# Feed-forward input blocks: hi and lo side by side as 512 moving columns, and 512-column lo pieces

## The chip, the cores and the metric

The kernel runs on one core of one Trainium2 chip. The time is the device time of one execution in microseconds (us); times of the kernel before are a median of three executions, and one further execution was profiled.

## What is computed

A sequence of 256 tokens with 1024 features, `x[256,1024]`, goes through 16 sub-layers, all in 32-bit floating point. Ten of them are feed-forward layers: eight gated ones with inner width 2816 (four) or 2752 (four), and two plain ones with inner width 4096. The others are six token mixers (a convolution, a gated linear recurrence, three kinds of attention, a pooling mixer).

```python
def swiglu_ffn(x, w_in, w_out):                      # 4 times (f00, f01, f10, f11), D_FF = 2816
    gate, up = jnp.split(x @ w_in, 2, axis=-1)
    return (jax.nn.silu(gate) * up) @ w_out

def swiglu(h, w_gate, w_up, w_down):                 # 4 times (g00, g01, g10, g11), D_FF_2 = 2752
    return (jax.nn.silu(h @ w_gate) * (h @ w_up)) @ w_down

...
x = x + jnp.square(jax.nn.relu(u @ w_ff1[i])) @ w_ff2[i]   # twice (m0, m1), width 4096
```

Between them stand the norms, the modulation by `ada_w` (its rows are called ada jobs below) and the residual sums.

## The kernel before

**Numbers.** Each fp32 factor is kept as two rounded parts, hi and lo, and a product is three matmuls: hi x hi, hi x lo and lo x hi. All weights lie in one DRAM tensor as chunks of [128, 2048] (1 MB), in the order of their use. `_load` fetches a chunk on SP's DMA queue into one of three `raw` buffers; `_split` makes `hi` on ACT (L330, four pieces of 512 columns) and `lo = raw - hi` on VectorE (DVE; L335). For the chunks of the feed-forward layers the lo comes in eight pieces of 256 columns (`LP = 8`), for all others in four of 512. There are five `hi` and five `lo` buffers, so a chunk can be split up to four chunks ahead of its use. The input of a layer lies transposed in two tiles `xh` and `xl` of [128, 8, 256]: features on the partitions, 8 slices of 128, 256 tokens.

**A feed-forward layer (`ffn`).** It has 22 input chunks U(f), each with the columns of gate and up for 128 hidden features, and 11 output chunks V(g). The first four U chunks are done by `first` into the four PSUM banks a0 to a3. The blocks f = 4 to 21 go through `u_products`: for the gate half and the up half (b = 0, 1) and each slice k there are three matmuls of 256 moving columns, in which the weights are the stationary factor and the input moves: `wh.xh` (L552), `wh.xl` (L553), `wl.xh` (L554). All 48 go into one PSUM bank, gate in the first half of it and up in the second, from the tag `ps` of two banks. `hidden` then empties the bank: Silu of the gate half on ACT (L733), times the up half on DVE (L734), and the split of the product into `hh` (ACT, L735) and `hl` (DVE, L736). In block f = 4, after the 40th matmul, `turn` puts in 8 transposes (L760) of the first four blocks' results, into two banks of the tag `tr` (also two banks), which `split` empties (L697, L698). After f = 5 the output products begin (`down`, L622, 512 moving columns of V, `hh` and `hl` stationary): V(0) and V(1) after f = 5, then one V after every second block to f = 15; the last six U blocks run back to back, and the last four V chunks follow in `finish`.

**A plain layer (`mlp`).** The same with 12 blocks through `proj_u` (which calls `u_products`), then Relu, square and split (L798, L799, L697, L698).

**Order.** The Tile framework places the instructions of each engine in a row at build time, by its own scheduling; on the chip each engine works off its row in order, and waits at its head. What follows an instruction in ACT's or DVE's row therefore waits with it. The ada jobs are 144 operations of DVE (L1159), strewn over seven of the gated layers.

Of the kernel before, what the change touches and what calls it, by code (L numbers as in the profile page):

```python
# [12 lines left out]
F32R = mybir.dt.float32r  # L13
# [278 lines left out]

class _K:
    RB, HB = 3, 5
    HP, LP = 4, 8

    def __init__(self, nc, tc, a, plan, stages, ctx):
        self.nc, self.tc, self.a, self.plan, self.stages, self.ctx = nc, tc, a, plan, stages, ctx
# [22 lines left out]
    def _split(self):  # L321
        i = self.nsplit
        while self.nload <= i:
            self._load()
        r = self.raws.pop(i)
        h = self.hi_p.tile([128, 2048], F32R, name="hi")
        l = self.lo_p.tile([128, 2048], F32R, name="lo")
        for p in range(self.HP):
            c = slice(2048 // self.HP * p, 2048 // self.HP * (p + 1))
            self.nc.scalar.activation(h[:, c], r[:, c], AF.Copy)  # L330

        lp = self.LP if self.plan[i][1][0] in "fg" or self.plan[i][1] in ("m0", "m1") else self.LP // 2
        for p in range(lp):
            c = slice(2048 // lp * p, 2048 // lp * (p + 1))
            self.nc.vector.tensor_tensor(l[:, c], r[:, c], h[:, c].bitcast(F32), op=OP.subtract)  # L335
        self.his[i], self.los[i] = h, l
        self.nsplit += 1
# [194 lines left out]
    def new_act(self):  # L532

        if self.the_act is None:
            self.the_act = (self.act.tile([128, 8, 256], F32R, name="xh"), self.act.tile([128, 8, 256], F32R, name="xl"))
        return self.the_act


# [6 lines left out]
    def u_products(self, w, act, p, nb=2):  # L545
        wh, wl = w
        xh, xl = act
        for b in range(nb):
            o = p[:, 256 * b:256 * b + 256]
            for k in range(8):  # L550
                c = slice(256 * k + 128 * b, 256 * k + 128 * b + 128)
                yield self.nc.tensor.matmul(o, lhsT=wh[:, c], rhs=xh[:, k, :], start=(k == 0), stop=False)  # L552
                yield self.nc.tensor.matmul(o, lhsT=wh[:, c], rhs=xl[:, k, :], start=False, stop=False)  # L553
                yield self.nc.tensor.matmul(o, lhsT=wl[:, c], rhs=xh[:, k, :], start=False, stop=(k == 7))  # L554

    def proj_tile(self, w, act, p, m, at):
        wh, wl = w
# [144 lines left out]
    def ffn(self, s, act):  # L702
        nc, tc = self.nc, self.tc
        nf = 22
        with tc.tile_pool(name="hp_" + s, bufs=2) as hp:
# [12 lines left out]
            def hidden(f, p):  # L718
                g, b = divmod(f, 2)
                if b == 0:  # L720
                    groups[g] = (hp.tile([128, 2, 256], F32R, name="hh", bufs=4), hp.tile([128, 2, 256], F32R, name="hl", bufs=4))
                hh, hl = groups[g]
                ragged = s[0] == "g" and f == nf - 1
                if ragged:

                    for t in (hh, hl):
                        nc.gpsimd.memset(t[64:, b].bitcast(F32), 0.0)
                n = 64 if ragged else 128
                gate = p[:n, :256]
                upp = p[64:128, :256] if ragged else p[:, 256:]  # L730
                sg = hp.tile([128, 256], F32, name="sg")
                h = hp.tile([128, 256], F32, name="h")
                nc.scalar.activation(sg[:n], gate, AF.Silu)  # L733
                nc.vector.tensor_tensor(h[:n], sg[:n], upp, op=OP.mult)  # L734
                nc.scalar.activation(hh[:n, b], h[:n], AF.Copy)  # L735
                nc.vector.tensor_tensor(hl[:n, b], h[:n], hh[:n, b].bitcast(F32), op=OP.subtract)  # L736

# [16 lines left out]

            def turn():
                for g in range(2):
                    p = self.ps("tr")
                    for b in range(2):
                        for m in range(2):
                            nc.tensor.transpose(p[:, 256 * b + 128 * m:256 * b + 128 * m + 128], hts[2 * g + b][:, m], self.ident)  # L760
                    groups[g] = self.split(p, hp)
# [3 lines left out]
            for g in range(2, 11):  # L765
                for f in (2 * g, 2 * g + 1):
                    w = self.take(("U", s, f))
                    if f > 4:
                        more()
                    p = self.ps()  # L770
                    products = self.u_products(w, act, p, 1 if s[0] == "g" and f == nf - 1 else 2)
                    if f == 4:
                        self.issue(products, 40, turn)
                    else:
                        self.issue(products)
                    hidden(f, p)
                    if f == 5:
                        acc = self.new_acc()
                    for j in ((0, 1) if f == 5 else (g - 1,) if f % 2 and g < 8 else ()):
                        w = self.take(("V", s, j))  # L780
                        more()
                        for m in range(2):
                            self.down(m, acc[m], w, hs(j), (128, 128), j == 0, False)
# [6 lines left out]
    def mlp(self, s, act):  # L790
        nc, tc = self.nc, self.tc
        with tc.tile_pool(name="hp_" + s, bufs=2) as hp:
            groups = {}

            def hidden(g, p):
                r = hp.tile([128, 512], F32, name="sg")
                h = hp.tile([128, 512], F32, name="h", bufs=1)
                nc.scalar.activation(r, p, AF.Relu)  # L798
                nc.vector.tensor_tensor(h, r, r, op=OP.mult)  # L799
                groups[g] = self.split(h, hp)  # L800

            hs = lambda g: [(groups[g][0][:, b], groups[g][1][:, b]) for b in range(2)]
            p4 = self.first(s, ((0, 1), (2, 3)), act)
            for g in range(4):
                r = hp.tile([128, 2, 256], F32, name="sg")
                h = hp.tile([128, 2, 256], F32, name="h", bufs=1)
                for m in range(2):
                    nc.scalar.activation(r[:, m], p4[g][m], AF.Relu)
                    nc.vector.tensor_tensor(h[:, m], r[:, m], r[:, m], op=OP.mult)
                groups[g] = self.split(self.turn4(h).rearrange("p b t -> p (b t)"), hp)  # L810
            acc = self.new_acc()
            self.rows_ahead(s)
            for g in range(2, 16):
                if g > 3:
                    hidden(g, self.proj_u(self.take(("U", s, g)), act))
                if g < 14:
                    w = self.take(("V", s, g - 2))
                    for m in range(2):
                        self.down(m, acc[m], w, hs(g - 2), (128, 128), g == 2, False)
            held = [(self.take(("V", s, g), g - 12), hs(g), (128, 128)) for g in (12, 13, 14, 15)]  # L820
            return self.finish(acc, held, self.cur_post)
# [1013 lines left out]
```

## Time and profile before

| | us |
|---|---|
| median of three executions | 2630.83 (2629.59 to 2634.77) |
| the profiled execution, its own time | 2628.67 |
| span of the profiled execution | 2626.9 |
| PE (TensorE matmul) busy | 2585.0 (98%) |
| DVE busy | 1914.4 (73%) |
| ACT busy | 1374.9 (52%) |

Spans and waits below are of the profiled execution. An operation's duration (mean ns of one) runs from its start to its end; successive operations on an engine overlap, so what one costs in a row of many is the distance from start to start. That distance is called pitch here, and it is shorter than the duration.

### The profile page before, as it was taken

To read this page: it belongs to the slowest core of one execution; us is meant where nothing else is said; L and a number is where in the kernel's file an instruction comes from. 1 tells how busy PE (TensorE), PEld (TensorE's weight loads), DVE (VectorE), ACT (ScalarE), POOL (GpSimd) and SP (SyncE) were. 2 spreads that over 40 slices of the span, in tenths; PEclk is the share of its full clock that TensorE was granted. 3 is DMA by queue.
4 is the path that set the end of the run, shared out by engine and by line. 5 is a ranking of instruction groups with operands and counts; after the bars stand their busy time and mean duration, and the time that the engine had idled before them with its cause. 6 is when DMAs were issued, how large, how long until landed. Compare 5 with 4: busy or idle time off the path is not lost.

```text
span 2626.9 us, 43032 instructions
## 1 busy us (share of the span) xinstructions
PE 2585.0 (98%) x15958; PEld 2286.7 (87%) x15958; DVE 1914.4 (73%) x5151; ACT 1374.9 (52%) x3037; POOL 71.6 (3%) x158
## 2 busy tenths in 40 slices
PE   8999999999999999999999999999999999999999
PEld 7998889989998899899779989977899788977898
DVE  7858587587578875985878778677855866577754
ACT  5545454454545544644664454466644655466543
POOL 0000000000000000000000000000100000000000
PEclk9999999999999999999999999999999999999999
DMA  8847376486425675784548768653555545542552
GB/s 325 305 161 281 145 259 246 150 331 233 169 92 194 258 288 177 279 307 175 177 162 303 264 230 332 219 210 129 210 191 177 187 162 197 187 170 97 192 182 91
DMA packets 92739, 554.53 MB, mean 211 GB/s; under 512 B 10717, under 2 KB 11757, under 8 KB 38385
## 3 DMA queue, kind: packets, MB, share of 16 engines
q1 hardware_dynamic: 92528, 551.79, 57.4%
q8 instruction: 125, 2.05, 0.3%
q14 instruction: 86, 0.70, 0.1%
HBM read 550.62 MB, written 1.13 MB: 210 GB/s over the span
## 4 chain that ended last, share of the span: by engine, by line
PE 58%; issue 34%; DVE 3%; ACT 2%; POOL 1%; DMA 1%; SPq 0%; POOLq 0%; ACTq 0%; DVEq 0%
PE a L622 20%; PE ps L552 8%; PE ps L553 8%; PE ps L554 8%; PE a L581 2%; PE a L583 2%; PE a L582 2%; DVE lo L335 2%; PE a L903 1%; PE tr L503 1%; DMA raw<-in_wall 1%; POOL ry L447 1%; ACT hi L330 1%; ACT junk L441 1%; PE a L1303 0%
## 5 line engine op out<-in xcount | busy, mean ns | idle before, releaser
L335 DVE TENSOR_TENSOR lo<-raw,hi 128x256 fp32r<-128x256 f32 (+1 forms) x2964 | 1158.1, 448 | 387.3 <-ACT hi L330 386.8
L330 ACT ACTIVATE hi<-raw 128x512 fp32r<-128x512 f32 x1652 | 944.3, 623 | 759.2 <-issue 271.3
L552 PE MATMUL ps<-xh,hi 128*128 128x256 f32 x2784 | 789.9, 284 | 0.0
L553 PE MATMUL ps<-xl,hi 128*128 128x256 f32 x2784 | 788.5, 283 | 0.0
L554 PE MATMUL ps<-xh,lo 128*128 128x256 f32 x2784 | 788.2, 283 | 0.0
L553 PEld LDWEIGHTS ps<-xl,hi 128*128 128x128 f32 x2784 | 533.4, 192 | 3.6
L552 PEld LDWEIGHTS ps<-xh,hi 128*128 128x128 f32 x2784 | 533.3, 192 | 3.6
L554 PEld LDWEIGHTS ps<-xh,lo 128*128 128x128 f32 x2784 | 533.4, 192 | 0.1
L622 PE MATMUL a<-hi,hh 128*128 128x512 f32 x960 | 309.6, 396 | 0.0
L622 PE MATMUL a<-lo,hh 128*128 128x512 f32 x960 | 309.3, 396 | 0.0
L622 PE MATMUL a<-hi,hl 128*128 128x512 f32 x960 | 309.3, 396 | 0.0
L622 PEld LDWEIGHTS a<-lo,hh 128*128 128x128 f32 x960 | 179.9, 188 | 43.7
L622 PEld LDWEIGHTS a<-hi,hl 128*128 128x128 f32 x960 | 179.9, 187 | 43.5
L1159 DVE SCALAR_TENSOR_TENSOR adaj<-adaw,cond 128x1024 bf16<-128x1024 f32 x144 | 175.6, 1219 | 42.8 <-DMA adaw<-in_ada 41.6
L622 PEld LDWEIGHTS a<-hi,hh 128*128 128x128 f32 x960 | 174.5, 188 | 36.2 <-ACT hh L697 0.2
L581 PE MATMUL a<-hi,xh 128*128 128x512 f32 x512 | 201.4, 394 | 3.2 <-ACT xh L511 1.8
L583 PE MATMUL a<-hi,xl 128*128 128x512 f32 x512 | 201.9, 396 | 0.6 <-DVE xl L512 0.6
L582 PE MATMUL a<-lo,xh 128*128 128x512 f32 x512 | 200.1, 391 | 0.3 <-DVE lo L335 0.3
L581 PEld LDWEIGHTS a<-hi,xh 128*128 128x128 f32 x512 | 96.6, 189 | 26.5 <-ACT xh L516 5.4
L583 PEld LDWEIGHTS a<-hi,xl 128*128 128x128 f32 x512 | 96.3, 188 | 24.7 <-DVE xl L512 3.2
L582 PEld LDWEIGHTS a<-lo,xh 128*128 128x128 f32 x512 | 96.6, 189 | 20.6 <-DVE lo L335 0.8
L735 ACT ACTIVATE hh<-h 128x256 fp32r<-128x256 f32 x144 | 59.1, 410 | 71.9 <-DVE h L734 71.9
(364 smaller groups left out, 2607.5 us busy)
## 6 DMA issues: line engine op xcount, KB each, us to landing
raw<-in_wall SPq DMA_DIRECT2D x413, 1024.0 KB, 4.8
adaw<-in_ada SPq DMA_DIRECT2D x144, 512.0 KB, 6.8
taps<-in_ctaps SPq DMA_DIRECT2D x10, 1024.0 KB, 7.8
G<-in_rows SPq DMA_DIRECT2D x16, 512.0 KB, 5.7
pg<-in_rows SPq DMA_DIRECT2D x12, 512.0 KB, 4.9
xn<-modd SPq DMA_DIRECT2D x12, 512.0 KB
cond<-condd SPq DMA_DIRECT2D x7, 512.0 KB, 6.1
memt<-in_mem SPq DMA_DIRECT2D x4, 512.0 KB, 3.3
```

The lines of the kernel that those rows point to most:

```text
L330: self.nc.scalar.activation(h[:, c], r[:, c], AF.Copy)
L335: self.nc.vector.tensor_tensor(l[:, c], r[:, c], h[:, c].bitcast(F32), op=OP.subtract)
L441: self.nc.scalar.activation(j, src, AF.Square, scale=1.0 / 32, accum_out=st[:, n:n + 1])
L552: yield self.nc.tensor.matmul(o, lhsT=wh[:, c], rhs=xh[:, k, :], start=(k == 0), stop=False)
L553: yield self.nc.tensor.matmul(o, lhsT=wh[:, c], rhs=xl[:, k, :], start=False, stop=False)
L554: yield self.nc.tensor.matmul(o, lhsT=wl[:, c], rhs=xh[:, k, :], start=False, stop=(k == 7))
L581: yield self.nc.tensor.matmul(p, lhsT=xh[:, k, t], rhs=wh[:, c], start=(k == 0), stop=False)
L582: yield self.nc.tensor.matmul(p, lhsT=xh[:, k, t], rhs=wl[:, c], start=False, stop=False)
L583: yield self.nc.tensor.matmul(p, lhsT=xl[:, k, t], rhs=wh[:, c], start=False, stop=(k == 7))
L622: mm = lambda l, r, i, st, sp: nc.tensor.matmul(acc[i], lhsT=l[:k, t], rhs=r[:k, 1024 * b + 512 * i:1024 * b + 512 * i + 512], start=st, s ...
L735: nc.scalar.activation(hh[:n, b], h[:n], AF.Copy)
L1159: self.nc.vector.scalar_tensor_tensor(junk, self.ada_w.pop(n), 1.0, self.cond, op0=OP.mult, op1=OP.mult, accum_out=self.mods[k][:, c:c + 1])
```

## The change

`xh` and `xl` become the two halves of one tile `both` of [128, 8, 2, 256], so that for each slice k the 512 columns [hi | lo] lie side by side. `wide_products` takes the place of `u_products` in the feed-forward blocks f = 4 to 21 and in the 12 blocks of each plain layer: for each half b and slice k one matmul of 512 moving columns, `wh` stationary (into the whole bank: the first 256 columns collect hi x hi, the others hi x lo), and one of 256 columns, `wl.xh`, into the first half of the bank. Gate and up therefore need a bank each: gate takes one of `ps`, up takes one of `tr`. `added` joins the halves of a bank: ACT copies the second to SBUF, DVE adds the first. `hidden` then works on SBUF: Silu (L754 in the new kernel), product (L756), split. The second bank of `turn` comes from `ps`, and `turn` stands after the 26th of now 32 products. The lo split is four pieces of 512 columns for every chunk. The blocks of the convolution, the recurrence and the first attention that go through `u_products` keep it.

```diff
--- before.py
+++ after.py
@@ -292,7 +292,7 @@
 class _K:
     RB, HB = 3, 5
-    HP, LP = 4, 8
+    HP, LP = 4, 4
     def __init__(self, nc, tc, a, plan, stages, ctx):
         self.nc, self.tc, self.a, self.plan, self.stages, self.ctx = nc, tc, a, plan, stages, ctx
@@ -328,8 +328,7 @@
         for p in range(self.HP):
             c = slice(2048 // self.HP * p, 2048 // self.HP * (p + 1))
             self.nc.scalar.activation(h[:, c], r[:, c], AF.Copy)
-
-        lp = self.LP if self.plan[i][1][0] in "fg" or self.plan[i][1] in ("m0", "m1") else self.LP // 2
+        lp = self.LP
         for p in range(lp):
             c = slice(2048 // lp * p, 2048 // lp * (p + 1))
             self.nc.vector.tensor_tensor(l[:, c], r[:, c], h[:, c].bitcast(F32), op=OP.subtract)
@@ -532,7 +531,8 @@
     def new_act(self):
         if self.the_act is None:
-            self.the_act = (self.act.tile([128, 8, 256], F32R, name="xh"), self.act.tile([128, 8, 256], F32R, name="xl"))
+            self.both = self.act.tile([128, 8, 2, 256], F32R, name="xh")
+            self.the_act = (self.both[:, :, 0], self.both[:, :, 1])
         return self.the_act
@@ -552,6 +552,28 @@
                 yield self.nc.tensor.matmul(o, lhsT=wh[:, c], rhs=xh[:, k, :], start=(k == 0), stop=False)
                 yield self.nc.tensor.matmul(o, lhsT=wh[:, c], rhs=xl[:, k, :], start=False, stop=False)
                 yield self.nc.tensor.matmul(o, lhsT=wl[:, c], rhs=xh[:, k, :], start=False, stop=(k == 7))
+
+    def wide_products(self, w, p):
+
+
+        wh, wl = w
+        mm = self.nc.tensor.matmul
+        for b, o in enumerate(p):
+            for k in range(8):
+                c = slice(256 * k + 128 * b, 256 * k + 128 * b + 128)
+                x = self.both[:, k]
+                hi = lambda start, stop: mm(o, lhsT=wh[:, c], rhs=x.rearrange("p i t -> p (i t)"), start=start, stop=stop)
+                lo = lambda: mm(o[:, :256], lhsT=wl[:, c], rhs=x[:, 0], start=False, stop=False)
+                if k < 7:
+                    yield hi(k == 0, False)
+                    yield lo()
+                else:
+                    yield lo()
+                    yield hi(False, True)
+
+    def added(self, out, p, n=slice(0, 128)):
+        self.nc.scalar.activation(out, p[n, 256:], AF.Copy)
+        self.nc.vector.tensor_tensor(out, out, p[n, :256], op=OP.add)
     def proj_tile(self, w, act, p, m, at):
         wh, wl = w
@@ -726,12 +748,12 @@
                     for t in (hh, hl):
                         nc.gpsimd.memset(t[64:, b].bitcast(F32), 0.0)
                 n = 64 if ragged else 128
-                gate = p[:n, :256]
-                upp = p[64:128, :256] if ragged else p[:, 256:]
                 sg = hp.tile([128, 256], F32, name="sg")
                 h = hp.tile([128, 256], F32, name="h")
-                nc.scalar.activation(sg[:n], gate, AF.Silu)
-                nc.vector.tensor_tensor(h[:n], sg[:n], upp, op=OP.mult)
+                self.added(sg[:n], p[0], slice(0, n))
+                nc.scalar.activation(sg[:n], sg[:n], AF.Silu)
+                self.added(h[:n], p[-1], slice(128 - n, 128))
+                nc.vector.tensor_tensor(h[:n], sg[:n], h[:n], op=OP.mult)
                 nc.scalar.activation(hh[:n, b], h[:n], AF.Copy)
                 nc.vector.tensor_tensor(hl[:n, b], h[:n], hh[:n, b].bitcast(F32), op=OP.subtract)
@@ -754,7 +776,7 @@
             def turn():
                 for g in range(2):
-                    p = self.ps("tr")
+                    p = self.ps(("tr", "ps")[g])
                     for b in range(2):
                         for m in range(2):
                             nc.tensor.transpose(p[:, 256 * b + 128 * m:256 * b + 128 * m + 128], hts[2 * g + b][:, m], self.ident)
@@ -767,10 +789,10 @@
                     w = self.take(("U", s, f))
                     if f > 4:
                         more()
-                    p = self.ps()
-                    products = self.u_products(w, act, p, 1 if s[0] == "g" and f == nf - 1 else 2)
+                    p = [self.ps(t) for t in (("ps",) if s[0] == "g" and f == nf - 1 else ("ps", "tr"))]
+                    products = self.wide_products(w, p)
                     if f == 4:
-                        self.issue(products, 40, turn)
+                        self.issue(products, 26, turn)
                     else:
                         self.issue(products)
                     hidden(f, p)
@@ -795,7 +817,9 @@
             def hidden(g, p):
                 r = hp.tile([128, 512], F32, name="sg")
                 h = hp.tile([128, 512], F32, name="h", bufs=1)
-                nc.scalar.activation(r, p, AF.Relu)
+                for b in range(2):
+                    self.added(r[:, 256 * b:256 * b + 256], p[b])
+                nc.scalar.activation(r, r, AF.Relu)
                 nc.vector.tensor_tensor(h, r, r, op=OP.mult)
                 groups[g] = self.split(h, hp)
@@ -812,7 +836,10 @@
             self.rows_ahead(s)
             for g in range(2, 16):
                 if g > 3:
-                    hidden(g, self.proj_u(self.take(("U", s, g)), act))
+                    w = self.take(("U", s, g))
+                    p = [self.ps(t) for t in ("ps", "tr")]
+                    self.issue(self.wide_products(w, p))
+                    hidden(g, p)
                 if g < 14:
                     w = self.take(("V", s, g - 2))
                     for m in range(2):
```

On PE, in block f = 4 of f01, the second feed-forward layer (`tr_` and `ps_` are PSUM banks, a new number is a new turn of a buffer). Before, the end of the 48 products with the transposes among them:

```order
L554 MATMUL ps_3636<-xh_84,lo_3621 128x256
L552 MATMUL ps_3636<-xh_84,hi_3620 128x256
L760 MATMUL tr_3677<-ident_94,hh_3594 128x128 x4
L760 MATMUL tr_3686<-ident_94,hl_3605 128x128 x4
L553 MATMUL ps_3636<-xl_85,hi_3620 128x256
L554 MATMUL ps_3636<-xh_84,lo_3621 128x256
```

And now, up to the first matmul of block f = 5:

```order
L566 MATMUL tr_3286<-xh_84,lo_3274 128x256
L782 MATMUL tr_3313<-ident_93,hh_3247 128x128 x4
L782 MATMUL ps_3322<-ident_93,hl_3258 128x128 x4
L565 MATMUL tr_3286<-xh_84,hi_3273 128x512
L566 MATMUL tr_3286<-xh_84,lo_3274 128x256
L565 MATMUL tr_3286<-xh_84,hi_3273 128x512
L566 MATMUL tr_3286<-xh_84,lo_3274 128x256 x2
L565 MATMUL tr_3286<-xh_84,hi_3273 128x512
L565 MATMUL ps_3369<-xh_84,hi_3349 128x512
```

Block f = 4 now holds two banks (ps_3285 before these rows, tr_3286) and the transposes two more, so that ps_3369 of block f = 5 is the buffer of ps_3285, and its tr_3370 that of tr_3286.

On ACT, at the same place, before (hi_3882 is the hi of U(6), a3 the fourth bank of `first`, and hh_3682 and hh_3691 empty the transposes):

```order
L751 ACTIVATE sg_3604<-a3_3544 128x128
L330 ACTIVATE hi_3882<-raw_3725 128x512 x2
L751 ACTIVATE sg_3610<-a3_3544 128x128
L330 ACTIVATE hi_3882<-raw_3725 128x512 x2
L697 ACTIVATE hh_3682<-tr_3677 128x512
L697 ACTIVATE hh_3691<-tr_3686 128x512
L330 ACTIVATE hi_3955<-raw_3808 128x512
L733 ACTIVATE sg_3705<-ps_3636 128x256
```

And now (hi_3497 is the hi of U(6)):

```order
L773 ACTIVATE sg_3257<-a3_3197 128x128
L330 ACTIVATE hi_3497<-raw_3359 128x512 x2
L773 ACTIVATE sg_3263<-a3_3197 128x128
L330 ACTIVATE hi_3497<-raw_3359 128x512 x2
L575 ACTIVATE sg_3339<-ps_3285 128x256
L754 ACTIVATE sg_3339<-sg_3339 128x256
L719 ACTIVATE hh_3318<-tr_3313 128x512
L719 ACTIVATE hh_3327<-ps_3322 128x512
L575 ACTIVATE h_3340<-tr_3286 128x256
```

The copies that empty the two banks of f = 4 stand behind the hi of U(6), and the second of them behind the two splits of the transposes. On DVE, now, the adds at the same place:

```order
L334 TENSOR_TENSOR lo_3498<-raw_3359,hi_3497 128x512 x2
L576 TENSOR_TENSOR sg_3339<-sg_3339,ps_3285 128x256
L334 TENSOR_TENSOR lo_3498<-raw_3359,hi_3497 128x512 x2
L1186 SCALAR_TENSOR_TENSOR adaj_3629,mods0_99<-adaw_3469,cond_3094 128x1024
L720 TENSOR_TENSOR hl_3319<-tr_3313,hh_3318 128x512
L720 TENSOR_TENSOR hl_3328<-ps_3322,hh_3327 128x512
L576 TENSOR_TENSOR h_3340<-h_3340,tr_3286 128x256
```

Between the two adds stand two lo pieces, an ada job and the two splits of the transposes.

On ACT, in block f = 4 of g00, the fifth feed-forward layer, now (hi_10381 is the hi of U(6), sg_10142 the last Silu of the blocks of `first`, whose product the transposes need):

```order
L773 ACTIVATE sg_10136<-a3_10076 128x128
L330 ACTIVATE hi_10381<-raw_10243 128x512 x3
L773 ACTIVATE sg_10142<-a3_10076 128x128
L330 ACTIVATE hi_10381<-raw_10243 128x512
L575 ACTIVATE sg_10223<-ps_10169 128x256
L754 ACTIVATE sg_10223<-sg_10223 128x256
```

Here that last Silu stands behind three pieces of U(6)'s hi.

## Rows read from the trace of the kernel before

**Rows 1.** The page: span, PE's line, and the granted clock by slice.

```profile
span 2626.9 us, 43032 instructions
...
PE 2585.0 (98%) x15958; PEld 2286.7 (87%) x15958; DVE 1914.4 (73%) x5151; ACT 1374.9 (52%) x3037; POOL 71.6 (3%) x158
...
PEclk9999999999999999999999999999999999999999
```

**Rows 2.** PE's waits by line: us in total, times, longest; the first row.

```profile
PE tr L503 <- DVE xn L488: 10.4, 3, 7.5
```

**Rows 3.** Two U-block stretches, line L552 alone: span; PE, PEld busy (count); PEclk; DMA; GB/s.

```profile
157.05:180.06 23.01, 18.08 (x64) 12.14 (x64) 1.00 0.53 184
...
1490.70:1513.70 23.00, 18.11 (x64) 12.16 (x64) 1.00 0.53 185
```

**Rows 4.** Timeline of PE at 2139 us, 512 columns: start, duration, engine, line, operands.

```profile
2139.68 0.39 PE L581 MATMUL a<-hi,xh 128*128 128x512 f32 x1
...
2147.61 0.39 PE L583 MATMUL a<-hi,xl 128*128 128x512 f32 x1
```

**Rows 5.** The chain that ended last, one V chunk: start, duration, engine, line.

```profile
105.86 5.60 PE a L622 x24
```

**Rows 6.** Groups by line and shape: busy us, mean ns of one | idle before, releasers.

```profile
L552 PE MATMUL ps<-xh,hi 128*128 128x256 f32 x2784 | 789.9, 284 | 0.0
...
L335 DVE TENSOR_TENSOR lo<-raw,hi 128x256 fp32r<-128x256 f32 x2624 | 939.4, 417 | 358.1 <-ACT hi L330 357.6
...
L335 DVE TENSOR_TENSOR lo<-raw,hi 128x512 fp32r<-128x512 f32 x340 | 218.9, 683 | 29.2 <-ACT hi L330 29.2
...
L734 DVE TENSOR_TENSOR h<-sg,ps 128x256 f32<-128x256 f32 x140 | 58.0, 414 | 4.9 <-ACT sg L733 4.6
...
L733 ACT ACTIVATE sg<-ps 128x256 f32<-128x256 f32 x140 | 51.5, 368 | 12.2 <-PE ps L554 12.2
```

**Rows 7.** A stretch of two U blocks and a V: PE, PEld, DVE, ACT, POOL.

```profile
1422.26:1439.40 17.14, 17.14 (x122) 16.01 (x121) 13.29 (x37) 8.26 (x17) 0.00 (x0) 1.00 0.67 243
```

**Rows 8.** Timelines of ACT and DVE, in U blocks back to back.

```profile
491.09 0.63 ACT L330 ACTIVATE hi<-raw 128x512 fp32r<-128x512 f32 x1 [2.99 <-PE ps L553]
...
491.75 0.43 DVE L335 TENSOR_TENSOR lo<-raw,hi 128x256 fp32r<-128x256 f32 x1 [2.32 <-ACT hi L330]
...
492.43 1.09 DVE L335 TENSOR_TENSOR lo<-raw,hi 128x256 fp32r<-128x256 f32 x3
```

**Rows 9.** Timelines of PE, ACT and DVE in block f = 4 of f01.

```profile
358.61 0.28 PE L552 MATMUL ps<-xh,hi 128*128 128x256 f32 x1
...
363.40 0.60 PE L760 MATMUL tr<-ident,hh 128*128 128x128 f32 x4
...
362.68 1.15 ACT L330 ACTIVATE hi<-raw 128x512 fp32r<-128x512 f32 x2 [3.26 <-DMA raw<-in_wall]
...
364.94 1.07 ACT L697 ACTIVATE hh<-tr 128x512 fp32r<-128x512 f32 x2
...
366.92 1.22 DVE L1159 SCALAR_TENSOR_TENSOR adaj<-adaw,cond 128x1024 bf16<-128x1024 f32 x1
...
369.33 1.28 DVE L698 TENSOR_TENSOR hl<-tr,hh 128x512 fp32r<-128x512 f32 x2
370.53 0.41 DVE L734 TENSOR_TENSOR h<-sg,ps 128x256 f32<-128x256 f32 x1
```

**Rows 10.** Timelines in block f = 4 of g00 and of g01: its first product, U(6)'s hi.

```profile
1086.55 0.28 PE L552 MATMUL ps<-xh,hi 128*128 128x256 f32 x1
...
1092.04 2.19 ACT L330 ACTIVATE hi<-raw 128x512 fp32r<-128x512 f32 x4 [3.51 <-DMA raw<-in_wall]
...
1381.60 0.28 PE L552 MATMUL ps<-xh,hi 128*128 128x256 f32 x1
...
1386.34 2.20 ACT L330 ACTIVATE hi<-raw 128x512 fp32r<-128x512 f32 x4 [1.33 <-DMA raw<-in_wall]
```

## The prediction

> **What bounds the kernel now.** I read the page first. PE is busy for 2585.0 of 2626.9 us and its granted clock is nine tenths or more in all 40 slices, the 2.4 GHz level [rows 1]. The view of waits by line says the same from the other side: PE's largest entry is 10.4 us in all, at the transposes of the norms [rows 2]. In the blocks that the change touches PE waits for nobody: in the windows of line L552 a U block runs at the same pace in f00 and in g10 [rows 3]. So the time is the sum of PE's pitches, and two questions remain: what the new matmuls cost from start to start, and whether the longer way out of PSUM makes PE wait.
>
> **The pitch.** In 23.01 us 64 groups of three matmuls start [rows 3]: 359.5 ns a group, 119.8 ns for 256 columns. For 512 columns the timeline at 2139 us has 35 pitches from 2139.68 to 2147.61 [rows 4]: 226.6 ns. The second 256 columns thus cost 106.8 ns (2.4 columns a ns, the granted level), and 13.0 ns are a fixed part that each instruction pays whatever its width. The change makes a group of three into a pair, 512 and 256 columns: 226.6 + 119.8 = 346.4 ns, 13.1 ns less. Of the 2784 groups [rows 6], 128 stay (convolution, recurrence, first attention); 2656 become pairs, and all lie on PE's row, which is the path: 2656 x 13.1 ns = **34.8 us less**. No column is saved, only the fixed part of 2656 instructions.
>
> The other end for the 512 columns is the V chunk in the chain, 24 matmuls in 5.60 us, 233.3 ns [rows 5]. By that the pair costs 353.1 ns and the gain is 6.4 ns x 2656 = 17.0 us. I take 226.6: there, too, one bank collects in succession, while the 233.3 stand with `hh` and `hl` as the stationary factor, and the U block's own stationary factor, a weight, has already shown the 13.0 ns at 256 columns.
>
> The Trainium skill, page "TensorE: Matmul & The Clock Gate", section "Back-to-back issue gap", gives the isolated gap as columns over 2.4 GHz plus 2.5 ns. Here the trace disagrees, with 13.0 ns left over at 256 and at 512 columns alike. By the page's figure 2656 instructions fewer would give 6.6 us, and the sum would be 2632 us.
>
> **VectorE and ACT.** A lo piece of 256 columns takes 417 ns, of 512 columns 683 [rows 6]; three of the narrow ones in a row take 1.09 us [rows 8], a pitch of 0.336, so the wide pitch is about 0.336 + 0.266 = 0.60. A chunk's lo falls from 2.69 to 2.41 us, 0.28 less in each of 328 chunks (2624 narrow pieces [rows 6]), 92 us of DVE. Against it stand 332 adds; the nearest row is the product of a 256-column PSUM half, 414 ns [rows 6], again some 0.336 in a row: 112 us. ACT gets 332 copies like its Silu of the same size, 368 ns [rows 6], some 0.26 in a row: 87 us. None of this is on the path. In the tightest kind of stretch, two U blocks and a V with ada jobs, DVE is busy 13.29 of 17.14 us [rows 7]; afterwards it is 13.29 - 0.84 + 4 x 0.336 = 13.8 of 17.14 - 0.42 = 16.7 us. In back-to-back U blocks ACT idles 2.99 us and DVE 2.32 us in each block, until PE gives back a hi buffer [rows 8]; the two copies (0.5) and two adds (0.7) fit. In these stretches a bank is wanted again only when the next block but one begins, a whole block of 5.5 us after its last matmul. I cost them at nothing; if that cover went, each tenth of a microsecond in the 168 blocks would be 17 us.
>
> **Block f = 5, the new wait.** Before, f = 5 took a fresh bank, and the bank of f = 4 could be emptied as late as 11.9 us after f = 4 began (370.53 - 358.61 [rows 9]). Now f = 4 and the transposes together use all four banks, so the first half of f = 5 needs the add of f = 4's gate half, and the second half needs that of its up half. Those stand behind the hi and lo of U(6) on ACT and DVE, whose chunk is still on its way. Queued behind the waiting copies are the hi pieces of the next chunk, and behind the waiting adds its lo; they are wanted two blocks later. PE would come to f = 5 at 16 x 346.4 ns plus 8 transposes of 0.11 us (from 363.40 on [rows 9], four in 0.43): 5.54 + 0.9 = 6.4 us after f = 4 began, and to its second half at 9.2.
>
> In f01 ACT gets U(6) at 362.68, is through it at 364.94, 6.3 us after 358.61 [rows 9], and copies: 6.7. DVE adds by 7.1, so PE waits 0.7. Then, on DVE, two lo pieces (1.2), the ada job (1.2, the row at 366.92), the two splits of the transposes (1.28 before, at 369.33 [rows 9]), the second add (0.4): 11.2, where PE wanted it at 9.2. Together **2.0 us**. In g00 U(6) comes 5.49 us after the block's start [rows 10], and three of its pieces now stand ahead of the last Silu that the transposes need. The transposes' last input is there at about 7.7 instead of 5.3, the first add at 9.1, and after an ada job, a lo piece and the two splits (1.2 + 0.6 + 1.2) the second is done at 12.5: 3.3 us. In g01 U(6) comes at 4.74 [rows 10], but the first copy stands between its pieces: 0.7. In the other five its hi comes earlier or the row has fewer steps; I put 2.0 for them together, an estimate between 0 and the 2.0 of f01 each. The sum is **8.0 us**, its bounds 3 (the first two alone, half as late) and 16 (all eight like f01). A gain is excluded, since before PE waited 0.0 us at L552 [rows 6].
>
> The plain layers have their transposes in the same tags and no ada jobs; I put them, and the slightly other order of PE between the layers, at 0, within 3 us either way, an estimate by the size of PE's waits at transposes [rows 2].
>
> **The sum.** 2628.67 - 34.8 + 8.0 = 2601.9 us for an execution like the profiled one; that one was 2.2 us under the median, so 2604 us on the median's scale. By the bounds of the wait and the 3 us beside it: 2596 to 2615.
>
> **Rivals.**
> - *No wait in f = 5.* The chunk U(6) comes earlier, since the faster blocks ahead and the wider lo pieces free `raw` buffers sooner. For it: in the rest of a layer the hi waits for PE and not for the DMA [rows 8]. Against it: the four blocks ahead of f = 4 are not changed. Time: 2604 - 8 = 2596. Chance 0.12.
> - *A larger wait*, all eight layers like f01, or the same at the plain layers' start: 16 instead of 8, 2612, up to 2616. For it: ACT's row holds the Silu behind U(6) in g00. Against: that chunk's arrival varies from layer to layer. Chance 0.13.
> - *512 columns at 233.3 ns*, as in the V chunks [rows 5]: 2604 + 17.8 = 2622. For it: that row is the commonest 512-column matmul of the kernel. Against: the 226.6 of rows 4. Chance 0.07.
> - *No fixed part to save.* The 13.0 ns go with the columns and not with the instruction, so that 512 in one piece cost what twice 256 cost, 239.6 ns; the gain is 0 and the wait stays: 2628.67 + 8.0 + 2.2 = 2639, slower. Against it stand the 35 pitches of 226.6 [rows 4], of another stationary factor. Chance 0.02. The page of the Trainium skill named above leans to this side, with its 2632 us.
> - *Slower: the emptying of the banks becomes the bound of every block.* ACT works off its row in order; the copy of the second half waits at its head for PE's last matmul, the add follows behind a lo piece that is now 0.27 us longer (683 against 417 ns [rows 6]). If that lateness reached PE in each of the 168 blocks it would cost 0.27 x 168 = 45 us: 2649. It decides from 0.19 us a block on (32 us, the 26.8 of the gain and the 0.2%). Against it stand the 2.99 and 2.32 us of idle time [rows 8] and the second bank of each tag. Chance 0.04.
>
> **How the numbers follow.** The forecast has 0.62, at 2604. The first three rivals with it are faster by more than 0.2% (5.3 us, about what a measurement of this kernel can tell from no change, so under 2625.6): 0.91 after 0.03 is kept back for the top of the third. Within 0.2%: 0.04, these 0.03 and the mild end of the last rival (0.01). Slower: 0.05, the rest of the last two. The range leaves out the last three rivals (0.13) and the lower tail of the first: 2594 to 2618.
>
> **What would show it.** In the windows of the new L565 within back-to-back U blocks 64 pairs should take 22.2 us (23.01 before); 22.6 would be the third rival. The waits of PE should have entries at L565 on the DVE adds L576 of about 8 us in all, in block f = 5 alone, the largest in g00 and f01. ACT and DVE should still idle in U blocks until PE returns a hi buffer; if instead PE's waits on L576 count in hundreds, the last rival holds. I would be wrong if the pair's pitch differed from 346 ns, since every nanosecond there is 2.7 us, or if the wait spread past f = 5.

## The result and the profile after

The new kernel took 2613.66 us, median of four executions (2607.84 to 2617.61), against 2632.8 us for the kernel before: a ratio of 0.9932, 95% interval 0.992 to 0.9943, 19 us faster. Measured a second time (e10 below) it was 2612.36 against 2630.93 us, 0.9931 (0.9918 to 0.9945). The forecast was 2604, range 2594 to 2618. The execution with the profile was the slowest of the first four, 2617.61 us.

The page of the new kernel, to be read beside [rows 1]: span, the busy line and the granted clock by slice.

```profile
span 2615.1 us, 37057 instructions
...
PE 2570.5 (98%) x13302; PEld 2153.1 (82%) x13302; DVE 1953.7 (75%) x4175; ACT 1504.6 (58%) x3373; POOL 72.4 (3%) x158
...
PEclk9999899999999999999999999999999999999999
```

PE has 2656 instructions less and is as full as before. The slice with an 8 lies in a token mixer. While PE had work, the granted clock stood at its 1.2 GHz level for 27 us of this execution, against 14 before and 20 in e10's profile, always outside the blocks that the change touches, after PE had been idle for part of the time; in the windows below it is at the 2.4 GHz level. DVE is 39 us busier (I had +20) and ACT 130 us (I had +87). The groups by line and shape show where:

```profile
L334 DVE TENSOR_TENSOR lo<-raw,hi 128x512 fp32r<-128x512 f32 x1652 | 1062.5, 683 | 157.9 <-ACT hi L330 154.1
L576 DVE TENSOR_TENSOR sg<-sg,ps 128x256 f32<-128x256 f32 x168 | 69.6, 414 | 7.8 <-ACT sg L575 3.2
L575 ACT ACTIVATE sg<-ps 128x256 f32<-128x256 f32 x168 | 64.0, 381 | 58.3 <-PE ps L565 55.7 <-DVE h L833 0.3
L754 ACT ACTIVATE sg<-sg 128x256 f32<-128x256 f32 x144 | 60.1, 418 | 101.8 <-DVE sg L576 101.8
```

The add costs the 414 ns that the nearest row of before promised [rows 6]; the copy takes 381 ns, and the Silu, which now reads SBUF, 418 instead of 368. None of it reaches PE in the steady blocks. In the blocks that run back to back ACT still waits for PE, at the copy of the up half, 1.42 us a block (2.99 before [rows 8]):

```profile
161.92 0.38 ACT L575 ACTIVATE h<-tr 128x256 f32<-128x256 f32 x1 [1.42 <-PE tr L565]
```

So the cover held. What did not come out is the pitch. The window of four back-to-back U blocks (span, PE, PEld, DVE, ACT, POOL, clock, DMA share, GB/s), 64 pairs of matmuls, beside the 23.01 us of before [rows 3]:

```profile
150.38:172.94 22.56, 22.56 (x129) 19.63 (x128) 15.68 (x32) 14.37 (x32) 0.00 (x0) 1.00 0.45 172
```

22.56 / 64 = 352.5 ns a pair, where I had 346.4 (22.2 us for the window). In the timeline of PE the pairs can be followed one by one:

```profile
150.38 0.40 PE L565 MATMUL ps<-xh,hi 128*128 128x512 f32 x1
150.61 0.28 PE L566 MATMUL ps<-xh,lo 128*128 128x256 f32 x1
150.72 0.40 PE L565 MATMUL ps<-xh,hi 128*128 128x512 f32 x1
150.96 0.28 PE L566 MATMUL ps<-xh,lo 128*128 128x256 f32 x1
151.07 0.40 PE L565 MATMUL ps<-xh,hi 128*128 128x512 f32 x1
151.31 0.28 PE L566 MATMUL ps<-xh,lo 128*128 128x256 f32 x1
151.43 0.40 PE L565 MATMUL ps<-xh,hi 128*128 128x512 f32 x1
```

From the start of a 512 to that of the 256 behind it are 0.23 to 0.24 us, from a 256 to the next 512 0.11 to 0.12. Averaged over the trace these are 235.6 and 117.4 ns: the 256-column matmul costs a little less than the 119.8 ns of before, the 512-column one 9 ns more than the 226.6 of rows 4. PE's waits that are new (the views list those of more than 0.15 us), from the timeline:

```profile
363.88 0.50 PE L565 MATMUL ps<-xh,hi 128*128 128x512 f32 x1 [0.26 <-DVE sg L576]
...
1091.71 0.33 PE L782 MATMUL ps<-ident,hl 128*128 128x128 f32 x1 [1.17 <-DVE hl L774]
...
1385.02 0.50 PE L565 MATMUL ps<-xh,hi 128*128 128x512 f32 x1 [0.96 <-DVE sg L576]
...
1876.82 0.50 PE L565 MATMUL tr<-xh,hi 128*128 128x512 f32 x1 [1.22 <-DVE ml L511]
...
2146.00 0.38 PE L566 MATMUL ps<-xh,lo 128*128 128x256 f32 x1 [0.30 <-DVE lo L334]
```

They are in the layers f01, g00, g01, g11 and m0, 3.9 us in all, where I had 8.0. The second half of f = 5 waits nowhere in this list. The section on the change has its bank wrong: the new kernel places it in the bank of the first transposes (tr_3370 in that of tr_3313), not in that of f = 4's up half (tr_3286). In f01 PE starts on it when the split of those transposes ends, before the add of the up half has begun:

```profile
366.09 0.68 DVE L720 TENSOR_TENSOR hl<-tr,hh 128x512 fp32r<-128x512 f32 x1
...
367.29 0.41 DVE L576 TENSOR_TENSOR h<-h,tr 128x256 f32<-128x256 f32 x1
```

```profile
366.83 0.50 PE L565 MATMUL tr<-xh,hi 128*128 128x512 f32 x1
```

With the measured terms the sum is 2628.67 - 2656 x 7.0 ns (18.6) + 3.9 = 2614.0, and with the 2.2 to the median 2616; measured were 2613.66 and 2612.36. From start to start in the traces, all U blocks with their transposes took 14.7 us less than before in this profile, which is the 18.6 less 3.9, and 18.5 less in e10's. The profiled execution itself took 2617.61, 3.6 us more than the 2614.0: that much was lost in other stages, where up to 7 us could come from the longer time at the 1.2 GHz level (an estimate, half of the 13.7 us more).

### The profile page after: what moved, and what is told of

Read it like the earlier page. It is cut to its first block, busy times and chain, and to the rows that moved or that the text cites. A ratio compares the mean times of both kernels' runs of the same rounds, so it can differ in the third digit from the quotient of the medians.

```text
span 2615.1 us, 37057 instructions
## 1 busy us (share of the span) xinstructions
PE 2570.5 (98%) x13302; PEld 2153.1 (82%) x13302; DVE 1953.7 (75%) x4175; ACT 1504.6 (58%) x3373; POOL 72.4 (3%) x158
## 4 chain that ended last, share of the span: by engine, by line
PE 57%; issue 35%; ACT 3%; DVE 3%; DMA 1%; POOL 1%; SPq 0%; POOLq 0%; ACTq 0%; DVEq 0%
PE a L644 20%; PE ps L565 8%; PE tr L565 8%; PE ps L566 4%; PE tr L566 4%; PE a L603 2%; PE a L604 2%; PE a L605 2%; PE a L930 2%; DVE lo L334 1%; ACT hi L330 1%; PE tr L502 1%; DMA raw<-in_wall 1%; ACT junk L440 1%; POOL ry L446 1%
## 5 line engine op out<-in xcount | busy, mean ns | idle before, releaser
L334 DVE TENSOR_TENSOR lo<-raw,hi 128x512 fp32r<-128x512 f32 x1652 | 1062.5, 683 | 157.9 <-ACT hi L330 154.1
L565 PE MATMUL ps<-xh,hi 128*128 128x512 f32 x1344 | 489.1, 398 | 1.2 <-DVE sg L576 1.2
L565 PE MATMUL tr<-xh,hi 128*128 128x512 f32 x1312 | 477.5, 398 | 1.2 <-DVE ml L511 1.2
L566 PE MATMUL ps<-xh,lo 128*128 128x256 f32 x1344 | 349.9, 281 | 0.3 <-DVE lo L334 0.3
L566 PE MATMUL tr<-xh,lo 128*128 128x256 f32 x1312 | 341.9, 281 | 0.0
L565 PEld LDWEIGHTS ps<-xh,hi 128*128 128x128 f32 x1344 | 252.7, 188 | 51.3 <-DVE sg L576 1.9
L565 PEld LDWEIGHTS tr<-xh,hi 128*128 128x128 f32 x1312 | 247.7, 189 | 45.2 <-DVE ml L511 1.5
L566 PEld LDWEIGHTS ps<-xh,lo 128*128 128x128 f32 x1344 | 253.9, 189 | 15.9 <-DVE lo L334 0.5
L566 PEld LDWEIGHTS tr<-xh,lo 128*128 128x128 f32 x1312 | 248.1, 189 | 15.0
L603 PE MATMUL a<-hi,xh 128*128 128x512 f32 x512 | 202.2, 396 | 3.1 <-ACT xh L510 1.9
L605 PE MATMUL a<-hi,xh 128*128 128x512 f32 x512 | 201.7, 395 | 0.0
L576 DVE TENSOR_TENSOR h<-h,tr 128x256 f32<-128x256 f32 x140 | 58.6, 419 | 150.7 <-ACT h L575 149.9
```

The lines of the kernel that those rows point to most:

```text
L565: hi = lambda start, stop: mm(o, lhsT=wh[:, c], rhs=x.rearrange("p i t -> p (i t)"), start=start, stop=stop)
L566: lo = lambda: mm(o[:, :256], lhsT=wl[:, c], rhs=x[:, 0], start=False, stop=False)
L576: self.nc.vector.tensor_tensor(out, out, p[n, :256], op=OP.add)
L603: yield self.nc.tensor.matmul(p, lhsT=xh[:, k, t], rhs=wh[:, c], start=(k == 0), stop=False)
L605: yield self.nc.tensor.matmul(p, lhsT=xl[:, k, t], rhs=wh[:, c], start=False, stop=(k == 7))
```

## Experiments: the pitch of the pair

Three theories of the missing 6 ns a pair. **A:** a 512-column matmul with a weight as the stationary factor costs 233 to 235 ns by itself, as the V chunks' 233.3 suggested [rows 5]; that was my third rival. **B:** it costs 226.6 ns, and what costs is that the width changes between neighbours. **C:** the fixed part of a pitch hangs on where the operands begin in SBUF. The addresses that the two programs were built with show a difference that no profile shows: the weight chunks, `xh` and `both` begin 32 bytes over a multiple of 64, `hh` and `hl` at a multiple of 64.

**e1, the 512-column matmuls alone.**

```diff
-                if k < 7:
-                    yield hi(k == 0, False)
-                    yield lo()
-                else:
-                    yield lo()
-                    yield hi(False, True)
+                yield hi(k == 0, k == 7)
...
-                        self.issue(products, 26, turn)
+                        self.issue(products, 13, turn)
```

> The new kernel without its 256-column matmuls (the term lo of the weight times hi of the input is left out), so that 512-column matmuls with a weight as the stationary factor stand back to back. The pair took about 353 ns in the new kernel instead of the 346.4 forecast. Theory A (each 512-column matmul of this kind costs its 233 to 235 ns by itself, as the V chunks' 233.3 do): the pitch here is 233 to 235 ns and a block of 16 lasts 3.74 us. Theory B (a 512-column matmul costs 226.6 ns, and the 6 ns come from the change of width between 512 and 256): the pitch is 226.6 ns and a block lasts 3.63 us.

One block of e1 in the timeline of PE:

```profile
94.73 1.98 PE L565 MATMUL ps<-xh,hi 128*128 128x512 f32 x8
96.54 1.98 PE L565 MATMUL tr<-xh,hi 128*128 128x512 f32 x8
```

Eight matmuls from 94.73 to 96.54: 226 ns each, and 227 in nearly all blocks of 16 (142 of 153); the others hold a wait or stand behind the transposes. A is out: the same instruction, with the same operands, costs 226.6 ns among its like and about 235 beside the 256 columns.

**e6, both weights times 512 columns.** This tells the change of width from the change between the hi and the lo buffer as the stationary factor.

```diff
-                lo = lambda: mm(o[:, :256], lhsT=wl[:, c], rhs=x[:, 0], start=False, stop=False)
+                lo = lambda: mm(o, lhsT=wl[:, c], rhs=x.rearrange("p i t -> p (i t)"), start=False, stop=False)
```

> The new kernel with the lo weight, too, times the 512 columns of hi and lo (adds the term lo times lo, 256 more columns a pair): hi and lo weights alternate as stationary factor as in the new kernel, but all matmuls are 512 wide. Theory B (the change of width costs): all at 226.6 ns, a block of 32 in 7.25 us. Rival B2 (the change between the hi and the lo buffer as stationary factor costs): 230 to 236 ns, a block 7.4 to 7.5 us.

Two blocks of e6, 64 matmuls:

```profile
171.22:185.72 14.51, 14.51 (x65) 12.01 (x64) 8.02 (x16) 7.20 (x16) 0.00 (x0) 1.00 0.32 114
```

14.51 / 64 = 226.7 ns. The stationary factor alternates as in the new kernel, and the surplus is gone; so it is the change of width. (The kernel took 2874 us, for the added columns.)

**e2, the same matmuls sorted by width within each bank.**

```diff
-            for k in range(8):
+            for part, k in [(0, k) for k in range(7)] + [(1, k) for k in range(8)] + [(0, 7)]:
                 c = slice(256 * k + 128 * b, 256 * k + 128 * b + 128)
                 x = self.both[:, k]
...
+                if part:
+                    yield mm(o[:, :256], lhsT=wl[:, c], rhs=x[:, 0], start=False, stop=False)
+                else:
+                    yield mm(o, lhsT=wh[:, c], rhs=x.rearrange("p i t -> p (i t)"), start=(k == 0), stop=(k == 7))
```

> The new kernel with the same matmuls in another order: in each bank the 512-column matmuls of slices 0 to 6 first, then all eight of 256 columns, then the last of 512. Widths change twice in a bank instead of 14 times. Theory A (the 512-column matmul's own cost): 233 to 235 and 118 to 120 ns stay, pair sum 352 to 354, time equal to the new kernel within 3 us, 2612 to 2616. Theory B (cost of changing width): pair sum about 347, 2656 x 6 = 16 us less than the new kernel, about 2598.

2601.53 us (2599.89 to 2604.87), ratio to the kernel before 0.9882 (0.9863 to 0.9902): 11 to 12 us under the new kernel, three quarters of the 16 expected. The same window and one bank of it in the timeline:

```profile
149.85:172.20 22.35, 22.35 (x129) 19.69 (x128) 15.69 (x32) 14.39 (x32) 0.00 (x0) 1.00 0.46 177
...
149.85 1.77 PE L568 MATMUL ps<-xh,hi 128*128 128x512 f32 x7
151.46 1.12 PE L566 MATMUL ps<-xh,lo 128*128 128x256 f32 x8
152.41 0.40 PE L568 MATMUL ps<-xh,hi 128*128 128x512 f32 x1
152.65 1.77 PE L568 MATMUL tr<-xh,hi 128*128 128x512 f32 x7
```

22.35 / 64 = 349.2 ns a pair, 3.3 less than with the widths mixed (8.8 us over 2656 pairs; PE's new waits were 1.4 us here, 2.5 less). The rest of the surplus stands behind the one change back to 512 columns that is left in a bank: the single 512 takes 0.24 us and the seven that follow 1.61, 230 ns each, where e1 has 226. Averaged over the banks of e2, the first five matmuls of 512 columns behind the 256s last 233, 236, 228, 232 and 231 ns from start to start, the others 227. Behind the change to 256 columns nothing is lost: the first two last 113 and 119 ns, the others 120. B holds, with the change from 256 to 512 alone as the one that costs. The price is not paid by one matmul: the next four pay too.

## Experiments: where the operands begin

**e3 and e4, aligned addresses in the new kernel and in the kernel before.**

```diff
         self.dram = pool("dramp", 1, space=bass.MemoryType.DRAM)
+        self.cst.tile([128, 8], F32, name="pad")
+        self.tiny.tile([128, 8], F32, name="pad2", bufs=1)
```

> The new kernel with two unused tiles of 32 bytes a partition, which move all weight chunks and the input tile from SBUF addresses that leave 32 over multiples of 64 bytes to multiples of 256 bytes; hh and hl, which lay at multiples of 64, now lie at multiples of 256. Nothing else changes. Theory C (the fixed part of a matmul's pitch hangs on where its two operands begin in SBUF): the pitch of the 512-column matmul and of the V chunks falls from 233 towards 227 or less, in all some 6 ns for each of 5800 matmuls of 512 columns, 20 to 40 us less. Theories A and B alike: no change, within 3 us of 2613.7.

> The kernel before with the same two unused tiles. Theory C: the V chunks' pitch falls from 233.3 towards 227, 6 ns for 2880 matmuls, 17 us less, and the 256-column pitch of 119.8 ns may fall too. Theories A and B: no change, 2632.8 within 3 us.

e3: 2595.9 us (2594.91 to 2599.11), ratio 0.9865 (0.9848 to 0.9882); measured once more as e12, 2595.92, 0.9862 (0.9849 to 0.9876).

> e3 once more, beside e11 on the same chip: 2596 within 3 us.

e4: 2617.35 us (2612.44 to 2621.13), ratio 0.9943 (0.9922 to 0.9965). So 17 us in the new kernel and 14 in the kernel before, from two unused tiles. The U blocks have no part in it (window of e3), the V chunks all (chain that ended last: new kernel, e3, e4):

```profile
149.04:171.60 22.56, 22.56 (x129) 19.64 (x128) 15.68 (x32) 14.39 (x32) 0.00 (x0) 1.00 0.47 178
```

```profile
105.59 5.59 PE a L644 x24
```

```profile
104.68 5.45 PE a L646 x24
```

```profile
105.55 5.47 PE a L624 x24
```

5.59 / 24 = 233 ns, 5.45 / 24 = 227 ns: 6 ns for 2880 matmuls, 17 us. C is right for the V chunks and wrong for the pair, whose operands lay alike before and after the move; so e3 stays under its 20 to 40 us, and the 256-column pitch of e4 did not fall.

With the addresses out of the way, e4 also shows B in a kernel that has no pairs, where a V chunk follows a U block of 256 columns:

```profile
105.27 0.28 PE L556 MATMUL ps<-xh,lo 128*128 128x256 f32 x1
105.39 0.63 PE L624 MATMUL a<-hi,hh 128*128 128x512 f32 x2
...
106.78 0.61 PE L624 MATMUL a<-hi,hh 128*128 128x512 f32 x2
...
110.86 0.28 PE L554 MATMUL ps<-xh,hi 128*128 128x256 f32 x1
```

The first six take 1.39 us, 232 ns each, the other 18 take 4.08, 227 each: the same price behind the same change.

**e7, `hh` and `hl` moved to where the chunks lie.**

```diff
         self.dram = pool("dramp", 1, space=bass.MemoryType.DRAM)
+        self.tiny.tile([128, 8], F32, name="pad2", bufs=1)
```

> The new kernel with one unused tile of 32 bytes a partition behind the weight chunks and the input tile, so that hh and hl lie 32 over a multiple of 64, as the weight chunks do in the kernel before and in the new one. Theory C1 (what counts for the V chunks is that stationary and moving operand lie alike within 64 bytes): their pitch falls from 233.5 to 227 ns, as in e3. Theory C2 (what counts is that the operands lie at multiples of 64): it stays at 233.5.

```profile
104.68 5.45 PE a L645 x24
```

Again 227 ns, with no operand of the V chunks at a multiple of 64; the one execution took 2600.15 us. Of the two distances tried, 0 and 32 bytes, what counts is that the stationary and the moving operand begin alike within 64 bytes (C1). This also explains why rows 4 and rows 5 differ: `xh` and the chunks lie alike, `hh` and the chunks did not. The 233.3 ns that I held out as the other end for the pair were a matter of the V chunks' addresses and had nothing to say of it.

## Experiments: the lo pieces, the waits, and the sum of the edits

**e8, lo in 256-column pieces again.**

```diff
-    HP, LP = 4, 4
+    HP, LP = 4, 8
...
-        lp = self.LP
+        lp = self.LP if self.plan[i][1][0] in "fg" or self.plan[i][1] in ("m0", "m1") else self.LP // 2
```

> The new kernel with lo in eight pieces of 256 columns again for the feed-forward layers. DVE has 0.28 us more for each of 328 chunks, 92 us of its busy time, off PE's path: no change of the time outside f = 5, where the hi and lo of U(6) come a little later: 2613.7, 0 to 3 us more. If the wide lo pieces were part of the gain, it would be more than 5 us slower.

2611.78 us (2611.72 to 2613.24), 0.9926 (0.9909 to 0.9942): the same as the new kernel. The wide lo pieces bring nothing that can be measured. One thing they do is seen in f01: ACT gets U(6) at 360.06, 3.1 us after the block's first matmul at 356.96, in e8 4.1 us after it (362.25 - 358.14), as before (4.07 [rows 9]). First the new kernel, then e8:

```profile
360.06 1.16 ACT L330 ACTIVATE hi<-raw 128x512 fp32r<-128x512 f32 x2 [2.62 <-DMA raw<-in_wall]
...
356.96 0.39 PE L565 MATMUL ps<-xh,hi 128*128 128x512 f32 x1
```

```profile
362.25 1.15 ACT L330 ACTIVATE hi<-raw 128x512 fp32r<-128x512 f32 x2 [3.28 <-DMA raw<-in_wall]
...
358.14 0.39 PE L565 MATMUL ps<-xh,hi 128*128 128x512 f32 x1
```

In the nine profiles with wide pieces and all matmuls (the new kernel, e2, e3, e5, e7, e9 to e12) the chunk came 0.7 to 3.3 us after the block's start in f01, in the three with narrow ones (before, e4, e8) 4.1 to 4.4. In g00 and g01 the arrival scatters from kernel to kernel in no such order.

**e10, the new kernel again.**

> The new kernel itself, for its time beside the others on the same chip: 2613.7 within 3 us by its first measurement. Its PE waits in f = 5 should again be near the 3.9 us of its first profile, not the 8.0 forecast, if they hang on when U(6) lands.

2612.36 us (2611.43 to 2613.84). PE's new waits were 0.9 us in g01, 1.2 in g11 and 0.3 in m0, 2.4 us and not 3.9; f01 and g00 had none. There U(6) came earlier than in the first profile: 2.2 us after the block's start in f01 (3.1) and 1.6 in g00 (3.8).

**e5 and e9, a whole block sorted by width, on aligned addresses.** e5 takes the 16 matmuls of 512 columns of both halves first, then the 16 of 256; e9 leaves block f = 4 sorted by bank.

```diff
+        for part in range(2):
+            for b, o in enumerate(p):
+                for k in range(8):
...
+                    if part:
+                        yield mm(o[:, :256], lhsT=wl[:, c], rhs=x[:, 0], start=False, stop=(k == 7))
+                    else:
+                        yield mm(o, lhsT=wh[:, c], rhs=x.rearrange("p i t -> p (i t)"), start=(k == 0), stop=False)
```

> The new kernel with two edits at once: the aligned addresses of e3, and the matmuls of a block sorted by width: the 16 of 512 columns of both halves first, then the 16 of 256, so that the width changes twice in a block instead of some 28 times (four times in e2). Theory B (each change of width costs PE some 3 ns in the matmuls that follow it; e2 took 12 us out by going from 14 changes a bank to two): the pairs fall to about 347.5 ns, 2656 x 5.5 = 14 us less than e3's 2595.9, about 2582, less 1 to 5 us of waits at the second half of f = 5, which is wanted a microsecond sooner: 2582 to 2587. If alignment and order did the same thing (one cause), the two don't add up and the time stays at 2596.

> As e5 (aligned addresses, a block's matmuls sorted by width), but block f = 4 of the gated layers finishes its gate bank first (8 of 512 and 8 of 256 columns, then the same for up), as e2 has it for every block. In e5 PE waited 5.7 us at the start of f = 5 for the add that empties the gate bank, which was complete only three quarters through the block. Theory: these waits fall to 1 or 2 us and the time by 4 us, to about 2590. If e5's missing gain (it was expected at 2582 to 2587 and took 2594) had another cause than these waits, the time stays at 2594.

e5 took 2594.22 us (2591.71 to 2596.33), 0.9857 (0.9842 to 0.9871), and e9 2595.22 (2591.57 to 2600.47), 0.9866 (0.9851 to 0.988): both missed, no better than e3 within the intervals. The pitch came: three of e5's blocks, 48 pairs, take 16.70 us, 347.9 ns a pair (first fence). PE's waits took part of it back; e5, then e9 (us in total, times, longest):

```profile
148.71:165.41 16.70, 16.70 (x98) 14.77 (x97) 11.76 (x25) 10.39 (x25) 0.00 (x0) 1.00 0.52 195
```

```profile
PE ps L569 <- DVE sg L573: 5.7, 4, 2.1
```

```profile
PE tr L573 <- DVE hl L721: 3.0, 6, 0.8
```

In e5 the gate bank of f = 4 is complete only three quarters through its block, and f = 5 waits for its add. In e9 that is mended, but f = 5 comes to its up bank after 1.8 us (the gate's eight matmuls of 512 columns) instead of 2.8, and waits for the split of the transposes whose bank it takes. Of the 7 to 12 us that e5 missed, these waits are 5.7; the rest is not settled, nor is e9's.

**e11, e2's order on e3's addresses.** If order and addresses are two causes, they add up.

> e2's order (each bank's 512-column matmuls of slices 0 to 6, then its eight of 256, then the last of 512) on e3's aligned addresses. If the order's gain (12 us in e2 against the new kernel) and the alignment's (17 us in e3) are two causes, they add up: about 2612.5 - 12 - 17 = 2583.5, and about 11 us under e12 in the same call; PE's waits in f = 5 stay near those of e2, under 2 us. If sorting by width gives nothing on aligned addresses (e5 and e9 came out at 2594 and 2595, beside e3's 2596), this is within 3 us of e12.

2585.34 us (2583.05 to 2587.29), ratio 0.9824 (0.9811 to 0.9838): 10.6 us under e12, measured beside it, and 27 under the new kernel's 2612.36, where e2 alone has 11 and e3 alone 16 to 17. They add up. PE's new waits, in full:

```profile
PE tr L570 <- DVE ml L513: 1.2, 1, 1.2
...
PE ps L570 <- DVE sg L574: 0.8, 1, 0.8
```

This is the fastest version: 47.6 us under the kernel before, two and a half times what the change brought.

## Why the prediction was right, and where its steps failed

*What bounds the kernel, and the direction:* right. PE's row is the path before and after, and the gain is that of fewer instructions on it, in the U blocks. e8 shows that the lo pieces are no part of it.

*The pitch of the pair, 34.8 us:* mis-sized; it measured 18.6. By its own sign the prediction was wrong here: it held itself wrong if the pair differed from 346 ns, and the window's 22.56 us is the 22.6 that it had named as the mark of the third rival. The step that failed is 226.6 + 119.8. Both numbers are right where they were read, each in a row of equal widths, and e1 and e6 give 226.7 for the very matmuls of the change. But the change puts the two widths in turn, which no row of before does: 352.5 ns, not 346.4. What there was of it before, the V chunks behind U blocks, is hidden by their addresses and comes out in e4. My third rival had nearly the right size, 353.1, with the wrong cause: the 512-column matmul does not cost 233 ns here by itself (e1), and the V chunks' 233 came from their addresses (e7).

*The page's rule:* the Trainium skill, page "TensorE: Matmul & The Clock Gate", section "Back-to-back issue gap", with its 2.5 ns for the isolated gap, would have given 2632, an estimate. The trace disagrees: 13.4 ns are left over at 512 columns (226.7) in e6, and 13.2 at 256 before [rows 3].

*VectorE and ACT, 0:* right, though their busy time rose more than the sum had it: it charged the pitch of a row, 0.336 and 0.26 us, for adds and copies that mostly stand alone and keep their engine busy for 0.41 and 0.38. That it was safe is seen in the 1.42 us that ACT still waits for PE in each back-to-back block.

*The wait in f = 5, 8.0 us:* half right. For the first half of f = 5 the mechanism and the places came as forecast (f01 and g01 at the add of the gate half, g00 at the transposes behind the last Silu). Two steps failed. One let the second half wait for the add of f = 4's up half, 2.0 us late in f01; that half takes the bank of the transposes, whose split is 1.2 us earlier there, and it waits in neither profile. The other took the arrival of U(6) from one execution of before. In f01 it comes about a microsecond sooner or more with the wide lo pieces, as the first rival said; elsewhere it scatters. Of the 3.9 us of the first profile and the 2.4 of the second, 1.2 were in no term: g11 waits in block f = 4 for the memory's transposed tiles, which share the tag `tr`, and not for an add.

*The sum:* 16.2 us too much gain in the pitch and 4.1 us too much wait partly cancelled, and 2604 became 2613.66. That this is inside the range is luck: with the pitch's error alone, 2604 + 16.2 = 2620 lies outside it.

*The slower rivals:* did not happen. PE waits on L576 twice in the profile, 1.2 us in all, not hundreds of times.

## What to carry to other kernels

A pitch read in a row of equal matmuls holds for such rows; before two kinds are put in turn, look for a place where they alternate, and if there is none, widen the bounds or measure one. Where a tuned kernel is bound by TensorE's pitch, its matmuls are best kept in runs of one width, and the addresses of stationary and moving tiles alike: these two, an order and 64 bytes, were worth more here than the change itself. A reordering that makes one bank complete later must be checked where banks are scarce; e5 and e9 lost part of their gain there.

## What the runs showed of the hardware

At the granted 2.4 GHz level a row of fp32r matmuls of 128 x 128 stationary columns starts every 119.8 to 120 ns at 256 moving columns and every 226.7 ns at 512, whichever weight buffer is stationary (e6). In turn they take 352.5 ns a pair, 6 ns more than the two; only the change from 256 to 512 costs: behind it five matmuls of 512 columns are 2 to 9 ns slower, 27 ns together, before the pitch settles (e2, e5, and e4's V chunks), while behind the change to 256 the first is some 7 ns faster (113 ns in e2). With the stationary operand beginning 32 bytes apart from the moving one, modulo 64, the 512-column matmul of the V chunks takes 233 ns without settling; alike it takes 227 whether both lie at a multiple of 64 (e3) or both 32 over it (e7). The Trainium skill, page "TensorE: Matmul & The Clock Gate", section "Step-by-step: what each phase is for", says that loading the next weights takes no SBUF read bandwidth from the running matmul, since each has a read port of its own. No run here measures that; e3, e4 and e7 show that where the stationary operand begins relative to the moving one changes the pitch all the same. What in the chip makes either cost, and whether they are one mechanism, no run here shows.
